# Moving modulation parts behind the spreads of two norms, and one chunk into the feed-forward

## The chip, the cores and the metric

The kernel runs on one core of one Trainium2 chip. A core has TensorE (matrix products), VectorE, ScalarE and GpSimd, each with its own queue of instructions, and queues for the transfers (DMA) that they and SyncE issue. In the profile these are PE (PEld is its weight load), DVE, ACT, POOL and SP. The metric is the device time of one execution in microseconds; the kernel before takes 1449.55 us, the median of three runs (1448.04 to 1452.1).

## The reference

The program computes two layers over 512 tokens (256 of a context, 256 of a latent) of width 1024, in float32. Layer 0 mixes tokens by latent attention, layer 1 by a gated DeltaNet; each is followed by a SwiGLU feed-forward. Both sub-layers of a layer are modulated and normed like this:

```
shift, scale, gate = chunks of (silu(c) @ w_mod + b_mod)
x = layer_norm(alpha * x + gate * sublayer(x * (1 + scale) + shift)) 
```

`w_mod` gives six chunks of 1024 per layer: shift, scale and gate for the mixer, and the same for the feed-forward, once for the latent's c and once for the context's. The modulation vectors depend on c alone, so they may be computed at any time before they are used.

## The kernel before

**Modulation parts.** A chunk (layer, number) of the modulation is cut into eight parts. A part is one transfer of 512 KB of `w_mod` (tile `mraw`, or two halves in tiles `raw`) and four matmuls of line 347 into `modps`; a profile row counts each of them twice, so a whole part shows as x8. After the eighth part ScalarE copies the sum (`modsb`, line 351), TensorE folds it by two small matmuls (line 354), and VectorE adds the bias (`modv`, line 356). `Chunks.step(n)` issues n parts. Each part's matmuls carry an order edge to the instruction in `env["gate"]`: they may not be issued ahead of it. Six `mraw` buffers hold loaded parts in the first norm gap.

**Matmuls in float32.** Every large product is three matmuls (lines 213 to 215) of high and low halves; the weights' halves are made on ScalarE (`whi`, line 185) and VectorE (`wlo`, line 186).

**The norm.** Residual rows are summed and squared as the sub-layer ends. TensorE brings the sums together (`lnstat`, line 424); `normalize` makes mean, variance and reciprocal root on VectorE (lines 464 to 467, and `rsqrt8`, 244 to 248), and `spread` (line 476) puts each of the two back over all partitions, by TensorE: `lnbc<-ident,lnmean` for the mean and `lnbc<-i_eighth,rs_y` for the root. Then the rows are finished: after the attention by `make_ops` (rstd line 549 on ScalarE, subtraction 559, multiplication 560, halves 552 and 553, h 583), after the feed-forward by `make_uh` (513, 514, 517 to 519, 522).

**Stages around the change.** The attention's output projection (`mo`) ends at 289 us; norm gap 1 and the making of operands follow, to about 340 us; the first feed-forward (`swiglu_wide`, seven products in place of eight) runs to 673 us; norm gap 2 follows, then the head of layer 1: the projection `head` (72 matmuls), whose result ScalarE copies out (`N<-head`, line 861) before the short convolutions on VectorE (`acc`, line 946) and the DeltaNet.

**What sets the order.** Each stage is written as a stream of instructions; a scheduler deals them to the engines' queues by a simulated timeline, and obeys the order edges. During the feed-forward, `MODS_RATE` = (1, 11) asks for one part for every eleventh fetch of weights. The gaps issue parts by hand: `FILL[1]` ahead of `normalize` and `FILL[2]` behind it, or `flush_mods()` for all that are left. Behind the feed-forward, all of chunk (1,2) and (1,3) are issued without regard to the spreads:

```
    env["mods"] = Chunks(chunks((1, 2), (1, 3)))
    mb, rs, ins = res.normalize()
    flush_mods()
```

Of the kernel before, what the change touches and what calls it, by code (L numbers as in the profile page):

```python
# [17 lines left out]
P = 128  # L18
# [57 lines left out]
HEADS = {0: 0, 1: 4, 3: 8}  # L76
URGENT = dict(scan=2000, base=1000, invert=700, last=3000, finish=700)
NORMS_FIRST = 500
MODS_RATE = (1, 11)
OUT_EARLY = 3  # L80
FILL = (6, 6, 6, 1)
WSUMS = 4
FFN0_AT = 25
FFN0_PARTS = ((0, 8), (8, 16), (16, 22))
# [12 lines left out]
def tile_trunk(ctx: ExitStack, tc: tile.TileContext, xT, params, consts, gconsts, wmod, w0, w1, out):  # L97
    nc = tc.nc
    V, S, G, PE = nc.vector, nc.scalar, nc.gpsimd, nc.tensor
# [4 lines left out]
    env = {}  # L104

    def open_pool(st, name, bufs=1, **kw):
        return st.enter_context(tc.tile_pool(name=name, bufs=bufs, reuse_waits="tile", **kw))
# [5 lines left out]
    def bank(name="bank", tag="bank"):  # L113
        tags = env["tags"]
        if tag not in tags:
            tag = next(t for t in ("bank", "ch", "pj") if t in tags)
        return env["ps"].tile([P, 512], F32, name=name, tag=tag, bufs=tags[tag])
# [94 lines left out]
    def mm3(ps_ap, a, b, first, last, **kw):  # L212
        PE.matmul(ps_ap, a[0], b[0], start=first, stop=False, **kw)  # L213
        PE.matmul(ps_ap, a[0], b[1], start=False, stop=False, **kw)  # L214
        return PE.matmul(ps_ap, a[1], b[0], start=False, stop=last, **kw)  # L215
# [14 lines left out]
    def linears(st, ps_aps, rhs):  # L230
        n = len(rhs)
        for k, r in enumerate(rhs):
            for p in ps_aps:
                mm3(p, st.take(), r, k == 0, k == n - 1)


    def rsqrt8(src, f, eps, n, pool):
# [122 lines left out]
    def chunks(*lc):  # L360
        return [(l, c, k) for l, c in lc for k in range(8)]

    def mods_in(pool, bufs, bufs2=1, tag="md", rows="mraw"):
        env["mraw"] = (pool, rows, bufs, "modsb", bufs2, tag)

    def flush_mods():
        env["mods"].step(96)
# [39 lines left out]
    class Residual:  # L407
# [65 lines left out]
        def spread(self, x, diag):  # L473
            bc = bank("lnbc", env["lntags"][1])
            for t in range(x.shape[1]):
                PE.matmul(bc[:, t * P:t * P + P], x[:, t:t + 1].to_broadcast([P, P]), diag, start=True, stop=True)
            return bc[:, 0:self.n]


# [45 lines left out]
    def new_u(shape=(P, NB, T)):  # L525
        return (bp.tile(list(shape), F32R, name="uhi", tag="uhi"), bp.tile(list(shape), F32R, name="ulo", tag="ulo"))

    def parts(u, n=NB, sl=slice(0, T)):
        return [(u[0][:, k, sl], u[1][:, k, sl]) for k in range(n)]
# [15 lines left out]
    def make_ops(r, mb, rs, ins, A, B, ops, pool, l, g, b, h):  # L545
# [5 lines left out]
        def part(src, hi, lo):  # L551
            x = S.activation(hi, src, AF.Copy)
            return x, V.tensor_tensor(lo, src, f32(hi), op=ALU.subtract)  # L553

        for k in range(4):
# [21 lines left out]
            part(t24, v[0][:, k], v[1][:, k])  # L577
            env["mods"].step(FILL[3])

# [145 lines left out]
    def swiglu(st, up, n, res, layer, streams, pool, nparts):  # L725
        k = NFF // nparts
        for q in range(nparts):
            hid = (pool.tile([P, k, n], F32R, name="hidh", tag="hidh", bufs=1),
                   pool.tile([P, k, n], F32R, name="hidl", tag="hidl", bufs=1))
            for f in range(0, k):  # L730
                if q == 0 and f < FFN_HEAD:
                    if f == 0:
                        head = [bank("pgu")[:, :n] for _ in range(2 * FFN_HEAD)]
                        linears(st, head, up)
                    pg, pu = head[2 * f:2 * f + 2]
                else:
                    pg, pu = bank("pg")[:, :n], bank("pu")[:, :n]
                    linear(st, pg, up)
                    linear(st, pu, up)
                sg = pool.tile([P, n], F32, name="sg", tag="sg", bufs=2)  # L740
                S.activation(sg, pg, AF.Silu)
                V.tensor_tensor(sg, sg, pu, op=ALU.mult)
                split(sg, hid[0][:, f], hid[1][:, f])
            hp_ = parts(hid, k, slice(0, n))
            if q == 0:
                if layer == 1:
                    flush_mods()
                g = gate(layer, 5)
            for m in range(NB):
                if q == nparts - 1 and m == NB - 2:  # L750
                    env["last"]()
                p = bank("ffo")
                linear(st, p[:, :n], hp_, res.count_sums if q == nparts - 1 and m == NB - 1 else None)
                res.add(p, g, m, streams, q == 0, q == nparts - 1)
# [3 lines left out]
    def swiglu_wide(st, ops, res, pool, rp, first):  # L758
# [16 lines left out]
        for q, (f0, f1) in enumerate(FFN0_PARTS):  # L775
            n, final = f1 - f0, f1 == NFF
            hid = (rp.tile([P, 8, T], F32R, name="hidh", tag="r"), pool.tile([P, 8, T], F32R, name="hidl", tag="hidl", bufs=1))
            for f in range(0, n, 2):
                if q == 0 and f == 2:
                    env["mods_rate"] = MODS_RATE  # L780
                    first(ins)
# [596 lines left out]
    st0, st1 = Stream(w0, plan), Stream(w1, [(i, h) for i in range(w1.shape[0]) for h in (0, 1)])  # L1378
# [10 lines left out]
    with tc.tile_pool(name="xin", bufs=1, reuse_waits="tile") as xp:  # L1389
        x0 = xp.tile([P, NB, T], F32, name="x0")  # L1390
        mods_in(xp, 8)
        u = new_u()
# [33 lines left out]
    res = Residual(Blocks(rp.tile([P, NB, T], F32, name="r", tag="r")), T, ln, Blocks(h))  # L1426
    op = parts(o)
    env["ffn"] = dict(wp=wq, raw=11, halves=True)
    for m in range(NB):
        p = bank("mo")  # L1430
# [6 lines left out]
    fx = ExitStack()  # L1437
    mods_in(open_pool(fx, "fx"), FILL[0], 1, "bank")
    env["mods"], env["mods_rate"] = Chunks(chunks((0, 5), (1, 0))), (0, 1)
    env["mods"].step(FILL[1])  # L1440
    mb, rs, ins = res.normalize()
    env["mods"].step(FILL[2])
    finish = make_ops(res.r, mb, rs, ins, A, B, ops, ln, 0, 0, 1, h)
    res = Residual(Blocks(h), T, ln, Blocks(h))
    flush_mods()
    mods_in(wq, 2)
    env["mods"], env["ahead"] = Chunks(chunks((1, 1), (1, 4))), 8
    wp1 = []

    def next_layer():  # L1450
# [11 lines left out]
    A, B = ln_mod(0, 2, 3, 1, 0, 1)  # L1462
    u = new_u()
    mods_in(wq, 5, 1, "md", "raw")
    env["mods"] = Chunks(chunks((1, 2), (1, 3)))
    mb, rs, ins = res.normalize()
    flush_mods()
    hl = dr.tile([P, NB, TS], F32, name="hl_dram")
    make_uh(res.r, mb, rs, ins, A, B, u, (0, 1), ln, 0, 2, 3, Blocks(h[:, :, 0:TS]), tok(1))
    nc.scalar.dma_start(out=hl, in_=h[:, :, 0:TS])  # L1470
# [1 line left out]

    env["wp"], env["ahead"], env["raw"], env["halves"] = wp1[0], 6, 2, False
    head = [bank("head") for _ in range(3)]
    linears(st1, head, parts(u))
    pb_.close()
    l0.close()
    pc = ExitStack()
# [6 lines left out]
    def latent():  # L1485
        return Blocks(*(big().rearrange("p (m t) -> p m t", m=4) for _ in range(2)))
# [6 lines left out]
    with tc.tile_pool(name="gdn", bufs=1, reuse_waits="tile") as pool:  # L1493
# [3 lines left out]
        res = Centred(latent(), TS, pool, env["base"], latent())  # L1497
        env["lntags"] = ("av", "ch")
        last(lambda m, p: res.add(p, g, m, (1,)))
        mb, rs, ins = res.normalize()  # L1500
    rp = open_pool(l1, "rp1")
    u = new_u()
# [9 lines left out]
    res = Residual(latent(), TS, rp, h)  # L1512
# [3 lines left out]
    mb, rs, ins = res.normalize()  # L1516
# [183 lines left out]
```

## Time and profile before

| | us |
|---|---|
| median of three runs | 1449.55 |
| the profiled execution | 1448.43 |
| its span | 1446.6 |
| TensorE busy | 1355.4 (94%) |
| VectorE busy | 981.6 (68%) |
| ScalarE busy | 742.9 (51%) |
| GpSimd busy | 220.5 (15%) |

The profiled execution is one execution; 1.83 us of its time lie outside the span. A row of the timeline has the start, the length of the group, the engine, the line, the operation with out<-in, and the count; in brackets stands how long the engine had been idle, and what released it. Rows on TensorE count passes, so a matmul in float32 of line 347 or 424 stands for two. The granted clock of TensorE is part of each window (1.00 is full).

### The profile page before, as it was taken

To read this page: it belongs to the slowest core of one execution; us is meant where nothing else is said; L and a number is where in the kernel's file an instruction comes from. 1 tells how busy PE (TensorE), PEld (TensorE's weight loads), DVE (VectorE), ACT (ScalarE), POOL (GpSimd) and SP (SyncE) were. 2 spreads that over 40 slices of the span, in tenths; PEclk is the share of its full clock that TensorE was granted. 3 is DMA by queue.
4 is the path that set the end of the run, shared out by engine and by line. 5 is a ranking of instruction groups with operands and counts; after the bars stand their busy time and mean duration, and the time that the engine had idled before them with its cause. 6 is when DMAs were issued, how large, how long until landed. Compare 5 with 4: busy or idle time off the path is not lost.

```text
span 1446.6 us, 27846 instructions
## 1 busy us (share of the span) xinstructions
PE 1355.4 (94%) x10753; PEld 1169.0 (81%) x10753; DVE 981.6 (68%) x2038; ACT 742.9 (51%) x1611; POOL 220.5 (15%) x329
## 2 busy tenths in 40 slices
PE   7999999999999999999798879898997998999996
PEld 4767687768989998987587768787886897899996
DVE  3355566869856865867699977678676656556665
ACT  3434444356634552552648546576576543755542
POOL 0000000040000000000007984925510000000000
PEclk9979999999999999999999889899999998999998
DMA  9444412665431332255247455354243243555651
GB/s 380 146 143 150 131 44 89 239 235 174 129 119 63 114 129 76 88 184 195 78 110 211 135 139 135 104 138 122 87 129 114 86 138 131 188 187 180 187 178 59
DMA packets 131692, 204.75 MB, mean 142 GB/s; under 512 B 70632, under 2 KB 72040, under 8 KB 131432
## 3 DMA queue, kind: packets, MB, share of 16 engines
q1 hardware_dynamic: 129656, 200.90, 43.6%
q10 hardware_dynamic: 1904, 2.08, 0.5%
q8 instruction: 84, 1.38, 0.4%
q14 instruction: 48, 0.39, 0.1%
HBM read 192.92 MB, written 10.03 MB: 140 GB/s over the span
## 4 chain that ended last, share of the span: by engine, by line
PE 74%; ACT 6%; DVE 5%; POOL 5%; DMA 5%; issue 4%; SPq 1%; ACTq 0%; POOLq 0%; DVEq 0%
PE ffo L214 4%; PE ffo L215 4%; PE ffo L213 4%; PE x L213 3%; PE x L214 3%; PE x L215 3%; PE modps L347 3%; POOL mt L1077 2%; POOL m L1078 2%; PE pw L1256 2%; DMA mraw<-in_wmod_dram 1%; PE pg L213 1%; PE y L213 1%; PE y L215 1%; PE y L214 1%
## 5 line engine op out<-in xcount | busy, mean ns | idle before, releaser
L186 DVE TENSOR_TENSOR wlo<-raw,whi 128x512 fp32r<-128x512 f32 x422 | 297.4, 711 | 204.9 <-ACT whi L185 185.8
L185 ACT ACTIVATE whi<-raw 128x512 fp32r<-128x512 f32 x422 | 262.8, 630 | 304.4 <-PE ffo L214 77.9
L214 PE MATMUL ffo<-hidl,whi 128*128 128x512 f32 (+1 forms) x352 | 119.2, 339 | 0.1
L215 PE MATMUL ffo<-hidh,wlo 128*128 128x512 f32 (+1 forms) x352 | 119.1, 338 | 0.0
L213 PE MATMUL ffo<-hidh,whi 128*128 128x512 f32 (+1 forms) x352 | 118.7, 341 | 0.0
L185 ACT ACTIVATE whi<-wsum 128x512 fp32r<-128x512 f32 x88 | 55.1, 631 | 60.9 <-PE x L214 26.7
L1077 POOL TENSOR_TENSOR mt<-m 128x31 f32<-128x31 f32 (+15 forms) x124 | 77.4, 625 | 9.0
L1078 POOL TENSOR_TENSOR m<-m,mt 128x31 f32<-128x31 f32 (+15 forms) x124 | 75.1, 606 | 9.2
L214 PEld LDWEIGHTS ffo<-hidl,whi 128*128 128x128 f32 x352 | 66.8, 190 | 8.2 <-DVE hidl L219 0.6
L213 PEld LDWEIGHTS ffo<-hidh,whi 128*128 128x128 f32 x352 | 66.7, 190 | 7.9 <-ACT hidh L218 0.4
L215 PEld LDWEIGHTS ffo<-hidh,wlo 128*128 128x128 f32 x352 | 66.8, 190 | 7.7
L186 DVE TENSOR_TENSOR wlo<-wsum,whi 128x512 fp32r<-128x512 f32 x88 | 59.8, 686 | 16.5 <-ACT whi L185 16.2
L213 PE MATMUL z<-uhi,whi 128*128 128x256 f32 x216 | 64.1, 297 | 5.4 <-DVE rs_t L246 5.3
L214 PE MATMUL z<-ulo,whi 128*128 128x256 f32 x216 | 64.6, 299 | 0.3 <-DVE ulo L553 0.3
L215 PE MATMUL z<-uhi,wlo 128*128 128x256 f32 x216 | 63.4, 293 | 0.0
L1168 POOL MEMSET XA<- 128x512 f32 x2 | 1.0, 526 | 363.4 <-DMA raw<-in_wmod_dram 363.4
L213 PE MATMUL v<-uhi,whi 128*128 128x512 f32 x128 | 52.8, 413 | 1.4 <-ACT whi L185 1.4
L1521 POOL TENSOR_TENSOR N<-N,mean 128x256 f32<-128x256 f32 x4 | 2.8, 722 | 336.4 <-DVE rs_t L247 336.4
L214 PE MATMUL v<-ulo,whi 128*128 128x512 f32 x128 | 53.1, 415 | 0.0
L560 POOL TENSOR_TENSOR r<-r,rstd 128x512 f32<-128x512 f32 x4 | 6.3, 1588 | 303.3 <-ACT rstd L549 302.6
L215 PE MATMUL v<-uhi,wlo 128*128 128x512 f32 x128 | 52.0, 407 | 0.0
L347 PE MATMUL modps<-mraw,cst 128*32 128x256 f32 x512 | 47.1, 427 | 3.7 <-DMA mraw<-in_wmod_dram 3.5
(473 smaller groups left out, 4294.8 us busy)
## 6 DMA issues: line engine op xcount, KB each, us to landing
raw<-in_w_dram SPq DMA_DIRECT2D x153, 512.0 KB, 3.6
mraw<-in_wmod_dram SPq DMA_DIRECT2D x80, 512.0 KB, 4.7
raw<-in_w_dram SPq DMA_DIRECT2D x138, 256.0 KB, 2.9
raw<-in_wmod_dram SPq DMA_DIRECT2D x32, 256.0 KB, 4.1
N<-g_dram SPq DMA_DIRECT2D x16, 512.0 KB, 4.2
x<-in_xT_dram SPq DMA_DIRECT2D x4, 512.0 KB, 10.2
h<-in_xT_dram SPq DMA_DIRECT2D x1, 2048.0 KB, 8.7
m<-g_dram SPq DMA_DIRECT2D x16, 128.0 KB, 4.7
```

What stands on the lines that cost most here:

```text
L185: S.activation(hi, src, AF.Copy)
L186: V.tensor_tensor(lo, src, f32(hi), op=ALU.subtract)
L213: PE.matmul(ps_ap, a[0], b[0], start=first, stop=False, **kw)
L214: PE.matmul(ps_ap, a[0], b[1], start=False, stop=False, **kw)
L215: return PE.matmul(ps_ap, a[1], b[0], start=False, stop=last, **kw)
L347: PE.matmul(p[32 * b:32 * b + 32, 0:TS], cst[:, k], w[b], start=k == 0, stop=k == 7, tile_position=(0, 32 * b))
L560: (V if fb < 4 else G).tensor_tensor(r[fb], r[fb], rs if fb == 0 else f, op=ALU.mult)
L1077: G.tensor_tensor(tv, m[:, 0:j, j:j + 1].to_broadcast([P, j, w]), m[:, j:j + 1, j:32].to_broadcast([P, j, w]), op=ALU.mult)
L1078: G.tensor_tensor(m[:, 0:j, j:32], m[:, 0:j, j:32], tv, op=ALU.subtract)
L1168: G.memset(X, 0.0)
L1256: PE.matmul(pw[:, e_ * P:e_ * P + P], N[d][:, 2 * c + e_], rr[:, e_], start=True, stop=True)
L1521: G.tensor_tensor(res.r[fb], res.r[fb], ms, op=ALU.subtract)
```

## The change

`spread` keeps its last matmul. In gap 1 two parts are issued ahead of `normalize` (six before), and five behind it with the last spread's matmul as gate; the parts that follow have the same gate. Chunk (1,3) leaves gap 2 and joins the feed-forward's list, with one part for every eighth fetch. In gap 2 the loads of five parts of chunk (1,2) are issued ahead of `normalize`, its parts have the last spread as gate, and those left after `step(5)` are issued behind the head's matmuls.

```
--- before.py
+++ after.py
@@ -76,9 +76,9 @@
 HEADS = {0: 0, 1: 4, 3: 8}
 URGENT = dict(scan=2000, base=1000, invert=700, last=3000, finish=700)
 NORMS_FIRST = 500
-MODS_RATE = (1, 11)
+MODS_RATE = (1, 8)
 OUT_EARLY = 3
-FILL = (6, 6, 6, 1)
+FILL = (6, 2, 5, 1)
 WSUMS = 4
 FFN0_AT = 25
 FFN0_PARTS = ((0, 8), (8, 16), (16, 22))
@@ -231,7 +231,8 @@
         n = len(rhs)
         for k, r in enumerate(rhs):
             for p in ps_aps:
-                mm3(p, st.take(), r, k == 0, k == n - 1)
+                ins = mm3(p, st.take(), r, k == 0, k == n - 1)
+        return ins
 
 
     def rsqrt8(src, f, eps, n, pool):
@@ -473,7 +474,7 @@
         def spread(self, x, diag):
             bc = bank("lnbc", env["lntags"][1])
             for t in range(x.shape[1]):
-                PE.matmul(bc[:, t * P:t * P + P], x[:, t:t + 1].to_broadcast([P, P]), diag, start=True, stop=True)
+                self.spreads = PE.matmul(bc[:, t * P:t * P + P], x[:, t:t + 1].to_broadcast([P, P]), diag, start=True, stop=True)
             return bc[:, 0:self.n]
 
 
@@ -1437,14 +1438,16 @@
     fx = ExitStack()
     mods_in(open_pool(fx, "fx"), FILL[0], 1, "bank")
     env["mods"], env["mods_rate"] = Chunks(chunks((0, 5), (1, 0))), (0, 1)
+
     env["mods"].step(FILL[1])
     mb, rs, ins = res.normalize()
+    env["gate"] = res.spreads
     env["mods"].step(FILL[2])
     finish = make_ops(res.r, mb, rs, ins, A, B, ops, ln, 0, 0, 1, h)
     res = Residual(Blocks(h), T, ln, Blocks(h))
     flush_mods()
     mods_in(wq, 2)
-    env["mods"], env["ahead"] = Chunks(chunks((1, 1), (1, 4))), 8
+    env["mods"], env["ahead"] = Chunks(chunks((1, 1), (1, 4), (1, 3))), 8
     wp1 = []
 
     def next_layer():
@@ -1462,9 +1465,13 @@
     A, B = ln_mod(0, 2, 3, 1, 0, 1)
     u = new_u()
     mods_in(wq, 5, 1, "md", "raw")
-    env["mods"] = Chunks(chunks((1, 2), (1, 3)))
+
+    env["mods"] = Chunks(chunks((1, 2)))
+    for _ in range(5):
+        env["mods"].load()
     mb, rs, ins = res.normalize()
-    flush_mods()
+    env["gate"] = res.spreads
+    env["mods"].step(5)
     hl = dr.tile([P, NB, TS], F32, name="hl_dram")
     make_uh(res.r, mb, rs, ins, A, B, u, (0, 1), ln, 0, 2, 3, Blocks(h[:, :, 0:TS]), tok(1))
     nc.scalar.dma_start(out=hl, in_=h[:, :, 0:TS])
@@ -1472,7 +1479,8 @@
 
     env["wp"], env["ahead"], env["raw"], env["halves"] = wp1[0], 6, 2, False
     head = [bank("head") for _ in range(3)]
-    linears(st1, head, parts(u))
+    env["gate"] = linears(st1, head, parts(u))
+    flush_mods()
     pb_.close()
     l0.close()
     pc = ExitStack()
```

In norm gap 1, on TensorE, these rows stood between the last statistics and the parts behind the second spread (a number behind a name tells buffers apart; 2685 is chunk (0,5), 2767 chunk (1,0)):

```order
L424 MATMUL lnstat_2610<-o_mean_67,lnsq_2647 128x1 x4
L347 MATMUL modps_2685<-mraw_2675,cst_74 32x256 x3
L347 MATMUL modps_2685<-mraw_2677,cst_74 32x256 x4
L347 MATMUL modps_2685<-mraw_2679,cst_74 32x256 x4
L347 MATMUL modps_2685<-mraw_2681,cst_74 32x256 x4
L347 MATMUL modps_2685<-mraw_2683,cst_74 32x256 x4
L476 MATMUL lnbc_2726<-ident_65,lnmean_2720 128x128 x4
...
L347 MATMUL modps_2685<-mraw_2696,cst_74 32x256
L476 MATMUL lnbc_2743<-i_eighth_69,rs_y_2732 128x128 x4
L347 MATMUL modps_2685<-mraw_2696,cst_74 32x256 x3
L347 MATMUL modps_2767<-mraw_2702,cst_74 32x256 x4
```

and now (2817 is chunk (1,0)):

```order
L425 MATMUL lnstat_2610<-o_mean_67,lnsq_2647 128x1 x4
L477 MATMUL lnbc_2702<-ident_65,lnmean_2696 128x128 x4
L477 MATMUL lnbc_2719<-i_eighth_69,rs_y_2708 128x128 x4
L348 MATMUL modps_2685<-mraw_2677,cst_74 32x256 x4
L348 MATMUL modps_2685<-mraw_2679,cst_74 32x256 x4
L348 MATMUL modps_2685<-mraw_2681,cst_74 32x256 x4
L348 MATMUL modps_2685<-mraw_2683,cst_74 32x256 x4
L348 MATMUL modps_2685<-mraw_2690,cst_74 32x256 x4
L348 MATMUL modps_2685<-mraw_2724,cst_74 32x256 x4
...
L348 MATMUL modps_2817<-mraw_2730,cst_74 32x256 x4
L213 MATMUL x_2916<-b110_2668,whi_2547 128x256
```

The two spreads stand next to each other right behind the statistics; the parts that lay ahead of and between them follow. Eleven parts now stand ahead of the first operand matmul `x`, two ahead of the spreads and nine behind; 15 did before. The line numbers of the new program are one higher from line 235 on.

In norm gap 2, on TensorE, before (7045 and 7115 are chunks (1,2) and (1,3)):

```order
L424 MATMUL lnstat_6957<-o_mean_67,lnsq_6981 128x1 x4
L354 MATMUL modps_7045<-ident_65,modsb_7106 128x8 x2
L476 MATMUL lnbc_7003<-ident_65,lnmean_6997 128x128 x4
L347 MATMUL modps_7115<-raw_7074,cst_74 32x256 x2
...
L347 MATMUL modps_7115<-raw_7111,cst_74 32x256 x2
L476 MATMUL lnbc_7020<-i_eighth_69,rs_y_7009 128x128 x4
L347 MATMUL modps_7115<-raw_7113,cst_74 32x256 x2
...
L347 MATMUL modps_7115<-raw_7138,cst_74 32x256 x2
L354 MATMUL modps_7115<-ident_65,modsb_7160 128x8 x2
L213 MATMUL head_7231<-uhi_6995,whi_6888 128x512
```

and now (7099 is chunk (1,2); the head's first and last row are in it):

```order
L425 MATMUL lnstat_7002<-o_mean_67,lnsq_7026 128x1 x4
L477 MATMUL lnbc_7077<-ident_65,lnmean_7071 128x128 x4
L477 MATMUL lnbc_7094<-i_eighth_69,rs_y_7083 128x128 x4
L348 MATMUL modps_7099<-raw_7051,cst_74 32x256 x2
...
L348 MATMUL modps_7099<-raw_7106,cst_74 32x256 x2
L213 MATMUL head_7198<-uhi_7049,whi_6933 128x512
...
L215 MATMUL head_7200<-uhi_7049,wlo_6964 128x512
L348 MATMUL modps_7099<-raw_7112,cst_74 32x256 x2
L348 MATMUL modps_7099<-raw_7114,cst_74 32x256 x2
L348 MATMUL modps_7099<-raw_7120,cst_74 32x256 x2
L348 MATMUL modps_7099<-raw_7122,cst_74 32x256 x2
L355 MATMUL modps_7099<-ident_65,modsb_7311 128x8 x2
L865 MATMUL batp_7352<-ident_65,N_7341 128x64 x4
```

The fold between statistics and spread is gone, both spreads stand together, 12 half parts remain ahead of the head, and four half parts and the fold come behind its last matmul. On ScalarE, at the end of `make_uh`, before:

```order
L522 ACTIVATE h_2287<-h_2287,par_63 128x256 x8
L1470 DMA hl_dram_7165<-h_2287 1024x1x256
L860 DMA N_7356<-in_gconsts_dram 128x768
L861 ACTIVATE N_7357<-head_7231 64x512
```

and now:

```order
L523 ACTIVATE h_2287<-h_2287,par_63 128x256 x8
L1477 DMA hl_dram_7132<-h_2287 1024x1x256
L352 ACTIVATE modsb_7311<-modps_7099 128x256
L861 DMA N_7340<-in_gconsts_dram 128x768
L862 ACTIVATE N_7341<-head_7198 64x512
```

The chunk's copy `modsb` stands behind the store of h and ahead of the load and the copy-out of the head. In the feed-forward 16 parts and two folds stand where eight parts, one fold and three half parts of chunk (1,2) stood. The instructions of layer 1 are the same in kind and number, but the scheduler deals many of them in another order; on VectorE, two `wlo`, two `acc`, one `QT` and five small ones more stand ahead of the first `m<-m,kkc`, and eight `acc` and two `wlo` more ahead of the second such pair.

More of the change, by code (lines that the diff above doesn't have):

```diff
@@ L78 @@
 NORMS_FIRST = 500
-MODS_RATE = (1, 11)
+MODS_RATE = (1, 8)
 OUT_EARLY = 3
-FILL = (6, 6, 6, 1)
+FILL = (6, 2, 5, 1)
 WSUMS = 4
@@ L233, in linears @@
             for p in ps_aps:
-                mm3(p, st.take(), r, k == 0, k == n - 1)
+                ins = mm3(p, st.take(), r, k == 0, k == n - 1)
+        return ins
     def rsqrt8(src, f, eps, n, pool):
@@ L475, in spread @@
             for t in range(x.shape[1]):
-                PE.matmul(bc[:, t * P:t * P + P], x[:, t:t + 1].to_broadcast([P, P]), diag, start=True, stop=True)
+                self.spreads = PE.matmul(bc[:, t * P:t * P + P], x[:, t:t + 1].to_broadcast([P, P]), diag, start=True, stop=True)
             return bc[:, 0:self.n]
@@ L1441, in tile_trunk @@
     mb, rs, ins = res.normalize()
+    env["gate"] = res.spreads
     env["mods"].step(FILL[2])
@@ L1446, in tile_trunk @@
     mods_in(wq, 2)
-    env["mods"], env["ahead"] = Chunks(chunks((1, 1), (1, 4))), 8
+    env["mods"], env["ahead"] = Chunks(chunks((1, 1), (1, 4), (1, 3))), 8
     wp1 = []
@@ L1464, in tile_trunk @@
     mods_in(wq, 5, 1, "md", "raw")
-    env["mods"] = Chunks(chunks((1, 2), (1, 3)))
+    env["mods"] = Chunks(chunks((1, 2)))
+    for _ in range(5):
+        env["mods"].load()
     mb, rs, ins = res.normalize()
-    flush_mods()
+    env["gate"] = res.spreads
+    env["mods"].step(5)
     hl = dr.tile([P, NB, TS], F32, name="hl_dram")
@@ L1474, in tile_trunk @@
     head = [bank("head") for _ in range(3)]
-    linears(st1, head, parts(u))
+    env["gate"] = linears(st1, head, parts(u))
+    flush_mods()
     pb_.close()
```

## The prediction, made before the change was timed

> **What bounds the kernel now.** I read the page first: busy shares, then the chain of work that ended last, then the group of the modulation matmuls.
>
> ```profile
> PE 1355.4 (94%) x10753; PEld 1169.0 (81%) x10753; DVE 981.6 (68%) x2038; ACT 742.9 (51%) x1611; POOL 220.5 (15%) x329
> PE 74%; ACT 6%; DVE 5%; POOL 5%; DMA 5%; issue 4%; SPq 1%; ACTq 0%; POOLq 0%; DVEq 0%
> L347 PE MATMUL modps<-mraw,cst 128*32 128x256 f32 x512 | 47.1, 427 | 3.7 <-DMA mraw<-in_wmod_dram 3.5
> ```
>
> TensorE is the bound over most of the span, so a modulation part (four matmuls of line 347, shown as eight rows) is free only where TensorE would wait anyway. The change moves parts between two such places, the norm gaps of layer 0, and a place that may have no room. So I looked at each of the three in the timeline and in a table of windows. Norm gap 1 on TensorE:
>
> ```profile
> 293.46 1.44 PE L424 MATMUL lnstat<-o_mean,lnsq 128*128 128x1 f32 x8
> 294.83 4.49 PE L347 MATMUL modps<-mraw,cst 128*32 128x256 f32 x38
> 299.25 1.88 PE L476 MATMUL lnbc<-ident,lnmean 128*128 128x128 f32 x8
> 302.05 1.16 PE L476 MATMUL lnbc<-i_eighth,rs_y 128*128 128x128 f32 x8
> 303.14 2.79 PE L347 MATMUL modps<-mraw,cst 128*32 128x256 f32 x40
> 308.32 0.38 PE L213 MATMUL x<-b,whi 128*128 128x256 f32 x1
> ```
>
> and the same gap on VectorE and ScalarE:
>
> ```profile
> 294.94 0.16 DVE L464 COPY lnmean<-lnstat 128x4 f32<-128x4 f32 x1 [5.03 <-PE lnstat L424]
> 297.51 0.16 DVE L248 SCALAR_TENSOR_TENSOR rs_y<-rs_t,rs_y 128x4 f32<-128x4 f32 x1
> 301.17 2.48 DVE L559 TENSOR_TENSOR r<-r,lnbc 128x512 f32<-128x512 f32 x4 [3.49 <-PE lnbc L476]
> 303.25 0.60 ACT L549 ACTIVATE rstd<-lnbc 128x512 f32<-128x512 f32 x1 [12.61 <-PE lnbc L476]
> 303.88 0.69 DVE L560 TENSOR_TENSOR r<-r,lnbc 128x512 f32<-128x512 f32 x1 [0.23 <-ACT rstd L549]
> 333.60 0.68 DVE L553 TENSOR_TENSOR t<-t,t 128x512 fp32r<-128x512 f32 x1
> ```
>
> The mean is ready at 295.10, but its spread runs at 299.25, behind 38 rows of parts; rs_y is ready at 297.67 and is spread at 302.05. VectorE and ScalarE stand still meanwhile. What follows in this stage (lines 549 to 583) keeps VectorE and ScalarE nearly full up to the last t at 333.60, so a start that is earlier there is an earlier end, if TensorE keeps up.
>
> ```profile
> 294.00:300.00 6.00, 6.00 (x46) 3.34 (x46) 2.29 (x14) 0.00 (x0) 0.00 (x0) 0.50 0.79 236
> 301.00:302.00 1.00, 1.00 (x14) 0.40 (x12) 0.83 (x2) 0.00 (x0) 0.00 (x0) 1.00 0.77 291
> 320.00:330.00 10.00, 8.61 (x76) 6.58 (x74) 9.23 (x12) 8.71 (x17) 8.33 (x8) 1.00 0.69 209
> 340.00:640.00 300.00, 300.00 (x2135) 279.59 (x2134) 220.58 (x349) 147.06 (x229) 0.00 (x0) 1.00 0.34 109
> ```
>
> These windows give TensorE's busy time first and its granted clock after the five engines. Two things matter: the clock is 0.50 from 294 to about 300.5, and in the feed-forward (340 to 640) TensorE is busy for 300.00 of 300.00 us, so there every part costs its full price.
>
> **Gap 1, the gain.** With the spreads ahead of the parts, the mean's spread starts at 295.15 and, at the 1.88 us it takes at the halved clock, ends near 297.0. VectorE is in the chain for rs_y until 297.67, so line 559 starts at 297.7 instead of 301.17 (3.5 earlier). The second spread runs from 297.9 to 299.8, ScalarE's rstd follows at 299.9 instead of 303.25, and line 560 at 300.5 instead of 303.88: 3.4 us. On VectorE the order also puts four small instructions of about 0.1 us each and one wlo behind the last t, so I take 4.0 us: the last t ends at 330.3 instead of 334.28.
>
> **Gap 1, what TensorE makes of it.** Two parts stand ahead of the spreads now and nine between the spreads and the first x, which needs TensorE itself. Price of a part: 40 rows in 2.72 us at full clock (303.14 to 305.86) are 0.545 us; 38 rows in 4.42 (294.83 to 299.25) are 0.93 at half clock. In the old kernel the clock came back about 5.7 us after the dense parts began. If that repeats from 299.8, five of the nine parts run at 0.93 and four at 0.545: 299.8 + 6.8 = 306.6, and with some wait for loads into the six buffers I take 306.9. The first x moves from 308.32 by 1.4, not by 3.4. Up to the old count of 24 parts, 13 instead of nine now fall into the stage behind the first x: four more, 3.0 us by the price below, of which 1.4 go into the idle time of 320 to 330. Then come these rows:
>
> ```profile
> 334.29 0.64 PE L347 MATMUL modps<-mraw,cst 128*32 128x256 f32 x8 [0.37 <-DMA mraw<-in_wmod_dram]
> 334.86 0.38 PE L214 MATMUL x<-t,whi 128*128 128x256 f32 x1
> 338.77 0.64 PE L347 MATMUL modps<-mraw,cst 128*32 128x256 f32 x8 [1.01 <-DMA mraw<-in_wmod_dram]
> 359.03 0.28 PE L214 MATMUL x<-b,whi 128*128 128x256 f32 x1
> 359.24 0.63 PE L347 MATMUL modps<-mraw,cst 128*32 128x256 f32 x6
> 359.80 0.39 PE L213 MATMUL x<-uhi,whi 128*128 128x256 f32 x1
> 610.96 0.51 PE L354 MATMUL modps<-ident,modsb 128*128 128x8 f32 x4
> 646.87 0.19 PEld L214 LDWEIGHTS ffo<-hidl,whi 128*128 128x128 f32 x1 [0.55 <-DVE hidl L219]
> ```
>
> Three parts of chunk (1,4) that stood at 330.03, 331.08 and 334.29 leave (1.7 us), with their DMA waits (0.37 at 334.29, as much at 331.08: 0.7). TensorE is then at the row of 334.86 at 334.86 - 1.4 + 3.0 - 1.4 - 1.7 - 0.7 = 332.7; VectorE would allow 330.3. The gain in hand is 2.2; the bounds are 1.0 (x held to 308.2, all nine parts at 0.93) and 4.6 (VectorE decides).
>
> **The feed-forward, the cost.** From that row on the old kernel does 6.5 parts (two of (1,4) by 339, three more by 506, one and a half at 645 to 651) and a fold; the new one does 16 and three folds, one of them of (1,1). 9.5 more parts. One alone among dense matmuls costs from 359.24 to 359.80, 0.56, and about 0.2 more: it starts 0.21 after the row of 359.03, and the row after 359.80 comes 0.22 later, where neighbours stand 0.12 apart otherwise. Together 0.75. Back to back it was 0.545. I take 0.68: 6.5 us, with 5.2 and 7.1 as bounds. Two more folds add 0.9 (0.44 each, taken from the 0.51 of 610.96 less its overlap). The wait of 1.01 for a load at 338.77 goes, and the last two parts now stand where TensorE's weight load waits 0.55 for hidl at 646.87. Sum: 6.5 + 0.9 - 1.0 - 0.55 = +5.85. At the end of the feed-forward the new kernel is then 5.85 - 2.2 = 3.6 us late.
>
> **Gap 2.** Its rows, on all engines:
>
> ```profile
> 675.08 0.69 DVE L451 TENSOR_TENSOR lnsqs<-lnsqs,lnsq 128x512 f32<-128x512 f32 x1
> 677.61 1.05 PE L424 MATMUL lnstat<-o_mean,lnsum 128*128 128x1 f32 x8
> 682.78 0.16 DVE L464 COPY lnmean<-lnstat 128x4 f32<-128x4 f32 x1 [7.01 <-PE lnstat L424]
> 683.46 2.05 PE L476 MATMUL lnbc<-ident,lnmean 128*128 128x128 f32 x8
> 685.98 0.16 DVE L248 SCALAR_TENSOR_TENSOR rs_y<-rs_t,rs_y 128x4 f32<-128x4 f32 x1
> 689.42 1.28 DVE L514 TENSOR_TENSOR h<-h,lnbc 128x512 f32<-128x512 f32 x2 [2.08 <-PE lnbc L476]
> 693.94 0.38 ACT L351 ACTIVATE modsb<-modps 128x256 f32<-128x256 f32 x1 [1.67 <-PE modps L347]
> 694.90 0.97 PE L213 MATMUL head<-uhi,whi 128*128 128x512 f32 x3
> 711.36 0.39 PE L215 MATMUL head<-uhi,wlo 128*128 128x512 f32 x1
> 712.09 0.59 ACT L861 ACTIVATE N<-head 64x512 f32<-64x512 f32 x1 [1.50 <-PE head L215]
> ```
>
> The sums are ready by 675.77, but the statistics start at 677.61 behind parts; they can go near 675.3, 2.3 us earlier, with lnmean at 680.5. From there rs_y takes 3.4 us now (682.78 to 686.14), with a chunk's end in between; without it I take 3.0, so 683.5. A spread at half clock takes 2.05: line 514 starts at 685.6 instead of 689.42, 3.8 earlier. The modsb that waits 1.67 ahead of the head's first uhi is gone too. Six parts remain ahead of the head: 685.6 plus six at 0.545 to 0.93 is 688.9 to 691.2; I take 690.0, 4.9 earlier. The gain is not all kept: two parts stand behind the head, and ScalarE's order has their modsb ahead of N<-head, so 711.75 (the end of the head's last row) - 4.9 + 1.14 for the parts, about 0.5 for modsb and 0.7 for a DMA issue behind it give N<-head at 709.3, 2.8 earlier (bounds 1.6 and 4.0). VectorE's convolutions of layer 1 are queued behind N<-head's ScalarE work, so this 2.8 reaches the mixer.
>
> **Layer 1** keeps its work, but the scheduler deals it anew. I price that at nothing; rival (c) gives the bounds.
>
> Sum against the profiled execution (span 1446.6, its own time 1448.43): 3.6 - 2.8 = +0.8, and about 0.3 back where the price of adjacent parts at the end of the feed-forward is 0.545: **+0.5**, 1448.9. The median of the runs is 1.1 above the profiled time, so 1450.0.
>
> **The clock, weighed.** The row of 294 to 300 shows 0.50 under dense parts. [...]
>
> **Rivals.** That the parts stay where they were is out, by the order shown above. (a) Faster: the clock is back before the parts behind the spreads, TensorE never holds VectorE, and parts fill holes at 0.545. Then 2.0 more in gap 1 (half of it by the clock), 1.3 in the feed-forward, 1.2 in gap 2 (head at 688.9): 0.5 - 4.5 = -4.0, with shorter spreads (1.16 for 1.88) -4.7: 1444.9. For it: TensorE does the parts anyway, and the old one lost 6 us at half clock under them. Against: 300.00 of 300.00.
> (b) The clock stays halved through both gaps' parts: nine at 0.93 end at 308.2 (+1.3), six end at 691.2 (+1.2): +3.0, 1452.5. For it: the 0.50 row.
> (c) Slower, through VectorE in layer 1:
>
> ```profile
> 765.92 0.79 DVE L1062 TENSOR_TENSOR m<-m,kkc 128x512 f32<-128x512 f32 x1
> 779.21 0.16 POOL L1073 MEMSET m<- 128x32 f32 x1 [9.19 <-DMA m<-scr]
> ```
>
> GpSimd's inversion starts at 779.21, after a wait of 9.19 for what VectorE made at 765.92. In the new order two wlo, two acc, a QT and five small ones more stand ahead of that instruction (2.6 us), and eight acc and two wlo ahead of the second such pair (6.1). If the inversion sets the pace, it is late by 2.6, and by up to 6.1 if the second pair does: +3.1 to +6.6, in the middle 1454.4. It decides once more than 3.9 of it survives. Against: the second pair has until the first inversion is over.
>
> **Chances.** Forecast 0.42, (a) 0.22, (b) 0.14, (c) 0.22. A change of less than 0.3% (4.35 us) cannot be told from none. Faster takes 0.19 of (a) and 0.05 of the forecast: 0.24. Slower takes 0.17 of (c), 0.03 of (b), 0.04 of the forecast: 0.24. The rest, 0.52, is no change. The range reaches from (a) to a little beyond the middle of (c): 1444 to 1455.
>
> **What would show it.** Right: line 559 near 297.7 and line 560 near 300.5; first x near 307; parts at 0.7 in the feed-forward and its end some 3.6 us later than 672.98; N<-head at the old time plus about 0.8. Wrong: the first x before 305.5 (then (a)), the clock still 0.50 at 306 (b), the inversion's first row later by more than N<-head's (c).

## The result, and the profile after

The changed kernel takes 1462.1 us in the median of five runs (1460.97 to 1465.09), the kernel before 1449.49 beside it: 1.0081 times as long, with a 95% interval of 1.0059 to 1.0103. It is slower by about 12 us, where the forecast was 0.5 us, as good as no change. The profiled execution has 1462.1 with a span of 1460.3, so 13.7 us more span than before.

In sum layer 0 went as the prediction says, layer 1 did not. Norm gap 1 on TensorE, after:

```profile
293.90 1.05 PE L425 MATMUL lnstat<-o_mean,lnsq 128*128 128x1 f32 x8
295.20 1.16 PE L477 MATMUL lnbc<-ident,lnmean 128*128 128x128 f32 x8 [0.25 <-DVE lnmean L465]
297.87 2.04 PE L477 MATMUL lnbc<-i_eighth,rs_y 128*128 128x128 f32 x8 [1.50 <-DVE rs_y L249]
299.84 4.14 PE L348 MATMUL modps<-mraw,cst 128*32 128x256 f32 x64
305.51 0.64 PE L348 MATMUL modps<-mraw,cst 128*32 128x256 f32 x8 [1.54 <-DMA mraw<-in_wmod_dram]
306.08 0.39 PE L213 MATMUL x<-b,whi 128*128 128x256 f32 x1
332.44 0.38 PE L213 MATMUL x<-t,whi 128*128 128x256 f32 x1
```

and on VectorE and ScalarE:

```profile
297.63 2.47 DVE L560 TENSOR_TENSOR r<-r,lnbc 128x512 f32<-128x512 f32 x4
299.94 0.60 ACT L550 ACTIVATE rstd<-lnbc 128x512 f32<-128x512 f32 x1 [8.54 <-PE lnbc L477]
300.57 0.69 DVE L561 TENSOR_TENSOR r<-r,lnbc 128x512 f32<-128x512 f32 x1 [0.47 <-ACT rstd L550]
332.28 0.68 DVE L554 TENSOR_TENSOR t<-t,t 128x512 fp32r<-128x512 f32 x1
```

The spreads stand alone right behind the statistics, the subtraction starts at 297.63 (301.17 before), rstd at 299.94 (303.25). But the last t is at 332.28, against 333.60: of the 3.5 us won at the start 1.3 are left at the end of the stage. Gap 2, after:

```profile
679.67 1.02 PE L425 MATMUL lnstat<-o_mean,lnsum 128*128 128x1 f32 x8 [0.63 <-DVE lnsum L451]
684.53 2.08 PE L477 MATMUL lnbc<-ident,lnmean 128*128 128x128 f32 x8 [0.25 <-DVE lnmean L465]
687.19 2.05 PE L477 MATMUL lnbc<-i_eighth,rs_y 128*128 128x128 f32 x8 [0.58 <-DVE rs_y L249]
689.16 4.86 PE L348 MATMUL modps<-raw,cst 128*32 128x256 f32 x48
693.96 0.97 PE L213 MATMUL head<-uhi,whi 128*128 128x512 f32 x3
711.92 0.38 ACT L352 ACTIVATE modsb<-modps 128x256 f32<-128x256 f32 x1 [2.24 <-PE modps L348]
712.37 0.59 ACT L862 ACTIVATE N<-head 64x512 f32<-64x512 f32 x1
```

N<-head, the door to layer 1, opens at 712.37; before it was 712.09. So **layer 0 as a whole costs 0.3 us, and the other 13.4 us are lost behind it**, in a layer whose instructions are the same. The first of these figures is no better than the spread of single executions: from the start of the last `mo` matmul, behind which the edits begin, to N<-head it is 423.0 us now and was 423.5, and four other programs whose layer 0 is that of before (runs 9 to 12 below) took 421.8 to 424.6 for it. The 13.4 us are far beyond that. The end of layer 1's mixer is the first matmul of its feed-forward (`pg`). From there to the end both kernels take 199 us. The groups of that matmul, first and last start behind the comma; before:

```profile
L213 PE MATMUL pg<-uhi,whi x160: 278/282/383, 1247.8 to 1364.2; 128*128 128x256 f32 x160
```

and after:

```profile
L213 PE MATMUL pg<-uhi,whi x160: 279/284/384, 1261.2 to 1377.5; 128*128 128x256 f32 x160
```

From N<-head to there it is 535.7 us before and 548.8 after. That stretch in windows, whole and from 330 us behind N<-head on (length; TensorE, its weight loads, VectorE, ScalarE and GpSimd busy; granted clock; DMA). Before:

```profile
712.09:1247.80 535.71, 480.54 (x4721) 418.80 (x4721) 392.05 (x915) 319.01 (x838) 195.12 (x296) 0.93 0.44 127
1042.09:1247.80 205.71, 186.03 (x1849) 166.04 (x1848) 133.18 (x351) 120.10 (x323) 6.83 (x8) 0.95 0.38 120
```

and after:

```profile
712.37:1261.20 548.83, 489.62 (x4726) 425.60 (x4726) 402.56 (x917) 317.73 (x838) 193.80 (x298) 0.91 0.43 123
1042.37:1261.20 218.83, 198.13 (x1867) 174.54 (x1865) 136.51 (x354) 120.48 (x326) 6.33 (x8) 0.91 0.37 116
```

TensorE does the same matmuls (4721 and 4726 records), but is busy 9 us longer and idle 4 us longer: the clock is 0.91 in place of 0.93. The second row has nearly all of it, 13.1 us more at a clock of 0.91 in place of 0.95. Length times what is missing of the clock is 10.3 us there before and 19.7 after.

### The profile page after: what moved, and what is told of

It is laid out like the page before. It is cut to its first block, busy times and chain, and to the rows that moved or that the text cites. A ratio compares the mean times of both kernels' runs of the same rounds, so it can differ in the third digit from the quotient of the medians.

```text
span 1460.3 us, 27828 instructions
## 1 busy us (share of the span) xinstructions
PE 1364.1 (93%) x10753; PEld 1175.1 (80%) x10753; DVE 989.0 (68%) x2038; ACT 741.2 (51%) x1611; POOL 216.6 (15%) x329
## 5 line engine op out<-in xcount | busy, mean ns | idle before, releaser
L1079 POOL TENSOR_TENSOR m<-m,mt 128x31 f32<-128x31 f32 (+15 forms) x124 | 78.7, 634 | 8.9
L348 PE MATMUL modps<-mraw,cst 128*32 128x256 f32 x576 | 51.3, 417 | 3.3 <-DMA mraw<-in_wmod_dram 3.3
```

The lines of the kernel that those rows point to most:

```text
L348: PE.matmul(p[32 * b:32 * b + 32, 0:TS], cst[:, k], w[b], start=k == 0, stop=k == 7, tile_position=(0, 32 * b))
L1079: G.tensor_tensor(m[:, 0:j, j:32], m[:, 0:j, j:32], tv, op=ALU.subtract)
```

## The experiments

Two theories stood against each other first. **ORDER**: the scheduler dealt layer 1 another order, and that order alone sets its time. **GATES**: the waits and the clock with which layer 0 hands over cost it. They can be told apart since several kernels with different edits to layer 0 were dealt the very same order of layer 1 (row by row on TensorE, VectorE, ScalarE and GpSimd, from the first rows behind the head on; up to three small rows at the very start, and one swapped pair of matmuls in one of the programs, are left aside), while edits to layer 0 that hardly differ were dealt different ones. The runs went over several chips, on which the kernel before has medians of 1449.5 to 1454.7; ratios are against the kernel before on the same chip.

**1. Gap 1 alone.** FILL, the gate and `res.spreads` as in the change; list, rate and gap 2 as before:

```
-MODS_RATE = (1, 8)
+MODS_RATE = (1, 11)
-    env["mods"], env["ahead"] = Chunks(chunks((1, 1), (1, 4), (1, 3))), 8
+    env["mods"], env["ahead"] = Chunks(chunks((1, 1), (1, 4))), 8
     (gap 2 and head as in the kernel before)
```

> Only the change of norm gap 1 (two parts ahead of the norm, five behind, gate on the last spread); the feed-forward's list and rate and gap 2 as before. Both theories: N<-head near 709 instead of 712.1, since gap 1 gave the new kernel some 3 us and no part moves into the feed-forward. Theory ORDER (layer 1 lost 13 us because the scheduler dealt it another order, and that order alone sets its time): from N<-head to the end of the span the time is that of its own order of layer 1, which is the one of the kernel with rate 7 in this batch, and equals that kernel's within 2 us; it may be anything from 734 to 748. Rival GATES (what layer 0 does, its waits and the state of the clock in which it hands over, costs layer 1 its time): gap 1 alone brings about half of the loss, 740 to 742 from N<-head to the end, total 1450 to 1452.

Measured: 1.0055 (1.0037 to 1.0074), slower. N<-head came at 710.77, 1.8 later than expected, and from there to the end it took 749.6, a little above ORDER's 734 to 748 and far above GATES' 740 to 742.

**2. Gap 2 and the moved chunk.** FILL and gap 1 as before, no gate there:

```
-FILL = (6, 2, 5, 1)
+FILL = (6, 6, 6, 1)
     mb, rs, ins = res.normalize()
-    env["gate"] = res.spreads
     env["mods"].step(FILL[2])
```

> Gap 1 as before; chunk (1,3) in the feed-forward at one part for eight fetches, gap 2 changed as in the new kernel. Both theories: N<-head near 715 to 716 (6.5 more parts in the feed-forward, 4.5 to 5, less 1.2 from gap 2). Theory ORDER: its layer 1 stands in the same order as that of the kernel with rate 9 in this batch, so both have the same time from N<-head to the end within 2 us. Rival GATES: about half of the loss, 740 to 742 from N<-head to the end, and less than the kernel with rate 9, which has both gaps changed.

Measured: 0.9947 (0.9929 to 0.9965), faster. N<-head came at 712.32, not at 715 to 716.

**3 and 4. The whole change with neighbouring rates.**

```
-MODS_RATE = (1, 8)
+MODS_RATE = (1, 9)        (run 3; (1, 7) in run 4)
```

> The whole change, but one part for every ninth fetch in the feed-forward in place of every eighth. Layer 0 is the new kernel's within 1 us (N<-head at 711.5 to 713.5). Theory ORDER: layer 1 stands in another order than in the new kernel, so its time differs from the new kernel's 748 by several us, and equals that of the kernel with gap 2 alone. Rival GATES: 748 from N<-head to the end and 1462 in all, as in the new kernel.

> The whole change, but one part for every seventh fetch. Layer 0 as the new kernel's within 1 us. Theory ORDER: from N<-head to the end equal within 2 us to the kernel with gap 1 alone, whose order of layer 1 it shares, and not 748. Rival GATES: 748 and 1462 in all.

Measured: rate 9 is faster than before, 0.9950 (0.9933 to 0.9967), though its N<-head at 716.21 is later than expected; rate 7 is slower, 1.0105 (1.007 to 1.0139). In between lies the change itself with rate 8, 1.0081. One step in the pace of a few background matmuls turns 0.5% faster into 1% slower.

**5. Gap 1 alone at rate 12.** As run 1, but

```
-MODS_RATE = (1, 11)
+MODS_RATE = (1, 12)
```

> Norm gap 1 alone changed, like the first run of the study, and one part for every twelfth fetch in place of every eleventh: eight parts in the feed-forward either way. Layer 0 as in that run: N<-head 421 to 423 us after the attention's last output matmul. ORDER: its layer 1 stands in the order of the two fast kernels (gap 2 with the move, and all with rate 9), so N<-head to the end takes 730 to 733 and not 749.6, and the whole is 0.4 to 0.8% faster than before. Rival GATES: as gap 1 alone, 0.5% slower than before.

Measured: 0.9931 (0.9904 to 0.9958), median 1441.05. This version beats both kernels. Run 1 has the same change to gap 1, and a rate that differs by one. Layer 0 was faster than expected: N<-head came 418.2 us behind the last `mo` matmul, not 421 to 423.

**6. The two late parts ahead of the head.**

```
-    env["mods"].step(5)
+    flush_mods()
...
-    env["gate"] = linears(st1, head, parts(u))
-    flush_mods()
+    linears(st1, head, parts(u))
```

> The whole change, but the last two parts of chunk (1,2) stand ahead of the head instead of behind it. Layer 1 stands in the new kernel's order. ORDER: N<-head to the end 746 to 750, total 1460 to 1464 on the first chip's scale, some 0.7% slower than before. In layer 0 the copy modsb no longer holds N<-head: the head's last matmul to N<-head 0.7 instead of 1.9, and the head begins up to 1.2 later. A theory in which the two parts and their copy behind the head are what delays layer 1 expects 735 to 738 from N<-head to the end.

Measured: 1.0070 (1.0049 to 1.0091). The two parts did not come ahead of the head but among its matmuls, which took 20.2 us from the first start to the last in place of 16.5. N<-head is at 712.33, so whether they stand there or behind the head makes no difference, and with nothing behind the head layer 1 is as slow as in the change. That the two parts behind the head delay layer 1 is out. The profiled execution of this run is a long one, 1467.8 against a median of 1460.7.

**7. The move alone**, no gate:

```
-MODS_RATE = (1, 11)
+MODS_RATE = (1, 8)
-    env["mods"], env["ahead"] = Chunks(chunks((1, 1), (1, 4))), 8
+    env["mods"], env["ahead"] = Chunks(chunks((1, 1), (1, 4), (1, 3))), 8
-    env["mods"] = Chunks(chunks((1, 2), (1, 3)))
+    env["mods"] = Chunks(chunks((1, 2)))
```

> Only chunk (1,3) goes into the feed-forward, at one part for eight fetches; no gate on the spreads, both gaps as the scheduler deals them. Feed-forward from the first operand matmul to its end 369 to 370 (before 364.4: 6.5 more parts and a fold at 0.7 each). Gap 2, feed-forward's end to head: with half the parts left and no gate 17 to 20 (before 22.2, with gate and move 14.3). ORDER: an order of layer 1 that no other run has, 728 to 750 from N<-head to the end; GATES: no gate, so 734 to 735 as before.

Measured: 1.0029 (1.0009 to 1.0049). From N<-head to the end it took 742.1: within what ORDER allowed, 7 us beyond what GATES had said.

**8. The gate of gap 2 alone**, both chunks there (`spread` keeps its last matmul as in the change):

```
     mb, rs, ins = res.normalize()
+    env["gate"] = res.spreads
     flush_mods()
```

> Only the gate in gap 2: both chunks stay there, all their parts behind the last spread. Feed-forward 364 to 365 as before. The spreads go right behind the statistics, so the head begins 15 to 17 after the feed-forward's end (before 22.2), but ten parts or so now fall between the head's matmuls: head 16.5 + 5 to 7. N<-head within 1.5 of before. ORDER: an order of layer 1 of its own, 728 to 750 from N<-head to the end; GATES: 738 to 742.

Measured: 1.0024 (1.0005 to 1.0042). N<-head moved more than expected, to 715.61: the head, with the parts among its matmuls, took 26.2 from its first to its last matmul in place of 16.5. Its order of layer 1 is not one of its own, as expected, but that of the kernel before: the matmuls and ScalarE's and GpSimd's rows are in the same order, and on VectorE one small row at the start (`N<-N`) stands three rows later. ORDER as stated for equal orders then asks for the time of before, and that is what was measured: 735.2 from N<-head to the end, against 734.5.

**What these eight say.** In the table, times are of the one profiled execution of each; "gap 1" is from the start of the last `mo` matmul to the first x, "feed-forward" from there to the start of the last `ffo`, "gap 2" from there to the first head matmul, "door" the start of N<-head. A letter stands for an order of layer 1; equal letters are equal orders.

| kernel | gap 1 | feed-forward | gap 2 | door | order | door to end | ratio |
|---|---|---|---|---|---|---|---|
| before | 19.7 | 364.3 | 22.2 | 712.09 | A | 734.5 | 1 |
| the change | 16.7 | 372.6 | 15.3 | 712.37 | B | 747.9 | 1.0081 |
| 6, all parts ahead | 15.7 | 373.8 | 14.1 | 712.33 | B | 753.8 | 1.0070 |
| 1, gap 1 alone | 16.1 | 366.9 | 21.2 | 710.77 | C | 749.6 | 1.0055 |
| 4, rate 7 | 16.3 | 372.8 | 16.5 | 712.12 | C | 750.3 | 1.0105 |
| 2, gap 2 and move | 20.7 | 369.3 | 14.3 | 712.32 | D | 731.8 | 0.9947 |
| 3, rate 9 | 16.7 | 373.3 | 17.6 | 716.21 | D | 730.5 | 0.9950 |
| 5, gap 1, rate 12 | 15.7 | 364.3 | 18.7 | 707.14 | D | 730.7 | 0.9931 |
| 7, move alone | 19.7 | 368.9 | 16.9 | 713.11 | E | 742.1 | 1.0029 |
| 8, gate of gap 2 alone | 19.9 | 364.8 | 18.4 | 715.61 | A | 735.2 | 1.0024 |

Order D takes 730.5 to 731.8 behind three different layers 0, one with both gaps changed and two with one each. Order C takes 749.6 and 750.3 behind two, and order A 734.5 and 735.2 behind two (734.4 to 736.4 with runs 9 to 11 below). Rates 7, 8 and 9 have gaps and a feed-forward within 2.5 us of each other, and 750, 748 and 730 behind the door. GATES expected 740 to 742 for runs 1 and 2, 748 for runs 3 and 4, as slow a time as run 1's for run 5, 734 to 735 for run 7 and 738 to 742 for run 8; only run 4 comes near, and GATES falls. N<-head itself missed its expectations by 2 to 3 us in runs 1, 2, 3, 5 and 8, so of layer 0 these runs show less than of layer 1. Order B is the one group with a spread, 747.9 and 753.8, since the execution profiled in run 6 lies 7 us above its median. Its last stretch:

```profile
1042.33:1267.20 224.87, 202.56 (x1866) 178.47 (x1864) 135.93 (x354) 120.66 (x326) 7.55 (x8) 0.89 0.37 114
```

That is the stretch of the change with the clock at 0.89 in place of 0.91: 24.7 us of missing clock in place of 19.7, for 6 us more.

**9 to 12. Are late inversions the price?** In the change GpSimd starts its first inversion at 782.32, 70.0 behind the door (67.1 before), and ends the third, inversion 2, 242.6 behind it (235.5 before). The prediction's slower rival (c) has the loss come from there. A theory LATE: the lateness goes through to the end.

```
             G.memset(dg, 2.0)
+            if g == 0:
+                for _ in range(6):        (12 in run 10; run 11 has g == 2 and 12)
+                    G.memset(dly, 0.0)
```

> The kernel before, with six GpSimd memsets of a scratch tile right behind the first row of inversion 0; every other instruction stands where it stood, on every engine. Inversion 0 ends some 3 us later (a memset of 128x512 took 0.53 in the profile of before). Theory LATE (the new kernel's layer 1 is long because GpSimd's inversions are late there, by 2.9 at the start of the first and 4.1 at its end): the lateness goes through to the end about one for one, +3 in total. Theory ORDER without it (what counts is which work TensorE has at hand when the scans run, not when the inversions come): the lateness is absorbed, total within 1.5 of before.

> The same with twelve memsets, some 6 us. LATE: +6 in total. ORDER without it: less than +3.

> Twelve memsets behind the first row of inversion 2 instead; in the new kernel inversion 2 ended 7.1 later than before, measured from N<-head. LATE: +6 in total, half of the new kernel's 13.4. ORDER without it: less than +3.

Measured: 0.9989 (0.9968 to 1.001), 1.0002 (0.9988 to 1.0015), 1.0001 (0.9984 to 1.0018). But these three did not do what they were made for. The scratch memsets do not wait for the inversion, and in the trace of run 10 they stand far ahead of the inversion, in idle time of GpSimd:

```profile
695.41 0.53 POOL L1076 MEMSET dly<- 128x512 f32 x1 [365.25 <-PE modps L347]
696.81 6.37 POOL L1076 MEMSET dly<- 128x512 f32 x11
```

So inversion 0 was not late, and they say nothing of LATE. They serve as a control: three more programs in order A on the other engines, 734.4, 736.4 and 735.8 from the door to the end.

Run 12 repeats the inversion's own first row, on the inversion's own tile:

```
-            G.memset(dg, 2.0)
+            for _ in range(27 if g == 2 else 1):
+                G.memset(dg, 2.0)
```

> The kernel before with the first row of inversion 2 (a memset of the matrix's diagonal, 0.16) repeated 26 times on the same tile, so that it cannot move ahead as the scratch memsets did: some 6 us of GpSimd in the inversion. Layer 1 stands as before up to that inversion; behind it the scheduler moves about a tenth of TensorE's rows. Inversion 2 ends 6 us later from N<-head than before (235.5), near 241 to 242, as late as in the new kernel (242.6). LATE: N<-head to the end 740 to 741 in place of 734.5, and the total 0.4% slower. ORDER without it: 732 to 737, total within 0.2% of before.

Measured: 0.9985 (0.9964 to 1.0007). This time the delay is there; two groups of the repeated rows and the end of the inversion, with N<-head at 714.03:

```profile
904.91 2.51 POOL L1074 MEMSET m<- 128x32 f32 x12
913.75 2.30 POOL L1074 MEMSET m<- 128x32 f32 x11
960.25 0.16 POOL L1080 MEMSET m<- 128x32 f32 x1
```

Inversion 2 ends 246.2 behind the door, 10.7 later than before and 3.6 later than in the change; inversion 3 ends at 327.8 (before 321.4, the change 326.6). The door to end took 737.9 in this execution, 3.4 more, and over ten runs there is no loss. With inversions at least as late as in the change, the 13.4 us do not appear. Inversions are late in order D too (the first starts 69.0 to 70.5 behind the door there), which is the fastest. LATE falls as the main cause. About 7% of TensorE's matmuls moved in this run as well (those outside the longest order that it has in common with the kernel before), so some lateness may have been covered by that.

**What is in the order.** The last stretch in order D, run 5:

```profile
707.14:1239.00 531.86, 481.08 (x4724) 417.48 (x4722) 392.11 (x915) 319.39 (x838) 195.38 (x296) 0.94 0.45 128
1037.14:1239.00 201.86, 187.90 (x1857) 166.98 (x1855) 136.24 (x354) 119.81 (x317) 5.35 (x8) 0.96 0.41 126
```

TensorE's idle time there and the clock that is missing come to 14.0 + 8.1 = 22.1 us, against 19.7 + 10.3 = 30.0 before and 20.7 + 19.7 = 40.4 in the change; the stretch is 201.9, 205.7 and 218.8 long. So in the slow order TensorE stands still or lacks clock for 10 us more than in order A, and in D for 8 less. Against the kernel before it is nearly all clock: the idle time is 20.7 in place of 19.7, but the clock is 0.50 in five stretches, some 37 us together, in place of three, some 20 us together. The clock is printed in hundredths, so each of these is good to 1 us or so. It is a book-keeping of where the time is, not of what put it there. The longest waits of TensorE for the scans' steps in that stretch (from 1037 to 1250 us; total, times, longest), in the change:

```profile
PE pw L1263 <- ACT w L1259: 3.9, 3, 1.9
PE ks L1249 <- DVE S L1268: 1.6, 2, 1.3
PE pw L1257 <- DVE rr L1254: 1.2, 1, 1.2
```

and in run 5:

```profile
PE ks L1249 <- ACT S L1265: 1.2, 1, 1.2
```

In the kernel before one wait for a convolution (`vt`) is the longest, and of those for the scans only one is over 1 us:

```profile
PE vt L1104 <- DVE th L949: 3.9, 1, 3.9
PE pw L1262 <- ACT w L1258: 1.3, 1, 1.3
```

`pw`, `ks`, `w`, `S` and `rr` are the steps of the scan, in which TensorE, ScalarE and VectorE wait for each other in turn. In the change TensorE more often has nothing else to do between them; the kernel before has as much idle time, but in other places. In the change the five stretches at 0.50 start at about 1079, 1113, 1127, 1222 and 1236, with 1.0 to 2.2 us of idle time in the 5 us ahead of each; but 2.4 us of idle time from 1097.4 to 1102.4 have no such stretch behind them before 1113. That the places of the idle time and of the clock at 0.50 are what makes order B slow is argued from these rows; no run changed it alone, and which rows of the order do it stays open.

## Why the prediction was wrong

The step that failed is the sentence on layer 1: "keeps its work, but the scheduler deals it anew. I price that at nothing". It was 13.4 us. The experiments show in its place that the order sets layer 1's time: the same work takes 730 to 754 us from N<-head to the end by the order that it is dealt. The forecast of 1450.0 lacks hardly anything else in sum, but that is luck, as the stages below show: N<-head was to open 0.5 to 0.8 later than before and opened 0.3 later.

- **Gap 1, the start.** Line 559 at 297.7, rstd at 299.9 and line 560 at 300.5 were predicted; 297.63, 299.94 and 300.57 were measured. Right.
- **Gap 1, what is kept.** TensorE was to be at x<-t at 332.7, and was at 332.44. This looks right and is not: the old kernel had done ten x<-t rows and two more x<-b rows by 334.86, at 0.12 each, which the prediction overlooked, so the gain in hand was 1.0, not 2.2.
- **The clock in gap 1.** It was to be halved behind the spreads until about 305.5, with first x at 306.9. The clock was back at 300.9 already, so the rows of 299.84 are eight parts in 4.14 us, mostly at full clock, and not five parts at half. First x came at 306.08 only, because the ninth part's load was waited for, 1.54 us where the sum had 0.3. With 0.49 us more behind the first x TensorE stood idle for loads for 2.0 us, and from 307.7 on the clock was 0.50. Single windows of the change:

```profile
298.00:299.00 1.00, 1.00 (x5) 1.00 (x6) 1.00 (x3) 0.00 (x0) 0.00 (x0) 0.50 0.00 0
301.00:302.00 1.00, 1.00 (x24) 0.60 (x20) 1.00 (x2) 0.70 (x2) 1.00 (x2) 1.00 0.16 20
304.00:305.00 1.00, 0.00 (x0) 0.00 (x0) 0.58 (x1) 1.00 (x4) 1.00 (x3) 1.00 0.79 262
310.00:311.00 1.00, 1.00 (x6) 1.00 (x6) 0.00 (x0) 1.00 (x3) 1.00 (x1) 0.50 1.01 397
315.00:316.00 1.00, 1.00 (x13) 0.45 (x11) 1.00 (x2) 1.00 (x3) 0.31 (x2) 1.00 1.01 406
```

  The clock is 0.50 from about 297.5 to 300.9 (3.4 us), and again from 307.7 to 314.5 (6.8 us), among the operand matmuls (windows of 0.1 us give these ends). That is a halved clock as in rival (b), at another place; that it is why only 1.3 us are left at the last t is argued, no run shows it.
- **The feed-forward.** It was to cost 5.85 behind that row. Its end moved from 672.98 to 679.0, so with 1.0 in hand it cost 7.0. With the other terms as they were, that is 0.8 for a part in place of 0.68. Pairs of runs do not settle it: 6.5 parts and a fold more cost 5.7 from run 1 to the change, 5.0 from the kernel before to run 2 and 4.6 to run 7, so 0.8, 0.7 and 0.6 for a part. That 0.68 was too low is not shown by them.
- **Gap 2.** From the end of the feed-forward to N<-head it is 33.4 in place of 39.1: 5.7 won, 2.8 forecast, beyond the bound of 4.0. The lnmean copy stands at 684.31, so 5.3 behind the feed-forward's end and not 7.5: the granted clock was 1.00 until 683.2, almost to the end of the statistics, while in the kernel before it was 0.50 from 679.7 on. The two parts behind the head cost less than was said: from the head's last start to N<-head it is 1.9 in place of 0.7, so 1.2 where the sum had 2.1.
- **Rivals.** At the end of the feed-forward the kernel was 2.4 later than forecast, and gap 2 won 2.9 more than forecast. These two errors cancel, so layer 0's sum came out right by luck. Of the rivals (c) named the place, layer 1, and the direction. Its price, 2.6 to 6.1 through late inversions, and its mechanism did not hold: the first inversion started 2.9 later behind the door, as it said, but order D has its first inversion 1.9 to 3.4 later at no loss, and run 12 the later ones.

What could have been seen ahead is that about one in seven of TensorE's matmuls in layer 1 stood at another place (by the longest order in common), and that nothing in the profile of before prices such a difference. With that, a range of 1444 to 1455 was too sure: the five orders here lie 730 to 754 behind the same door.

## What to carry to other kernels

Where a scheduler deals the whole program, an edit in one stage is also a new draw for every later stage; look at the order of the stages that were not edited, and where it differs, widen the range by what such draws have been worth (20 us of 535 here), not by the cost of the edit. To learn what an edit itself is worth, time it behind the same later order, or stage by stage; by that measure gap 1's edit wins 3 to 4 us at its first x, and gap 2 is shorter by 5 to 8 us with gate and move, but the feed-forward takes most of it back. From the last `mo` matmul to N<-head the change, runs 1, 2, 4, 6 and 7 take 421.7 to 424.3, no less than unchanged layers 0 do (421.8 to 424.6). Only run 5 is clearly ahead with 418.2; rate 9 is behind with 426.4, and gap 2's gate without the move (run 8) with 428.5. A draw is also an offer: gap 1's edit at rate 12 takes 0.9931 of the old time. In the profiled execution some 5 us of that lie in layer 0 and some 4 us in order D; why layer 0 gains so much more there than in run 1 stays open.

## What was not expected of the hardware

In gap 1 two waits of 2.0 us together were followed by 6.8 us at a clock of 0.50. The last matmuls of `w` in it (from 313.45 on) start 0.21 apart, those of `y` right behind it, at 1.00, 0.12 apart. Half of the 6.8 us, 3.4, is an estimate from the clock of the most that TensorE loses there, and it is more than the waits. The same order of layer 1 differs between executions, and the clock with it: order B in two executions took 747.9 and 753.8, at a clock of 0.91 and 0.89 in the last stretch. Ten runs of run 9's kernel lie between 1443.9 and 1455.8 on one chip, wider than the 4.35 us that were taken as the bound of what can be told apart; only medians of several runs, on the same chip, told these kernels apart.
